# Bias tiles on GpSimd's queue and low-rank weights one head pair earlier, in a two-layer hybrid attention kernel

## The chip, the cores and the metric

The kernel runs on one core of one Trainium2 chip. The metric is device time in microseconds of one execution, as the median of several runs. The engines named below are PE (TensorE, matrix products and transposes), DVE (VectorE), ACT (ScalarE), POOL (GpSimd) and SP (SyncE). SP computes nothing here: it issues transfers, in the order of its instruction stream. POOL both computes and issues transfers.

## The reference

Two layers over 512 latent tokens on a grid 64 wide and 256 context tokens, all of width 1024, in float32. Layer 0 has two groups of eight heads side by side: latent attention with low-rank queries and keys, and two-dimensional neighbourhood attention. Layer 1 has sliding-window attention. Each layer ends in a SwiGLU. The part in which the change lies, cut to what matters:

```
p = modulate(h) @ w_in
# neighbourhood heads: softmax over near latent keys and all context keys
s_lat = q @ k_near * scale + rel_bias[:, row offset, column offset]   # outside the window: -1e30
s_ctx = q @ k_ctx * scale
o_na  = softmax([s_ctx, s_lat]) @ [v_ctx, v_near]
# latent heads
q = rms_norm(p[:, :256], q_norm) @ w_q_up          # 8 heads of 64 + 32 (rotated)
c = rms_norm(p[:, 256:384], kv_norm)
o_mla = softmax((q_nope @ w_uk @ c + q_rope @ k_rope) * scale) @ c @ w_uv
```

## The kernel before

Activations lie with features on partitions and 768 tokens (512 latent, 256 context) along the row. A float32 product is made from three products of high and low parts: `load_w` (L301) fetches a weight into a buffer `wr`, lets ACT write the high part `wh`, and DVE, or POOL where an engine is given, subtract it for the low part `wl`. The transfer is on SP in each case; only the subtraction follows that argument.

After the input projections (`projections`, L1010) the neighbourhood heads run as four pairs p = 0 to 3 (`na_jobs`, L1157). A pair has three jobs: context queries, latent query blocks 0 and 1, blocks 2 and 3. `attend` (L652) runs the front of a job (scores, `take` at L536 with the bias and the row minimum on DVE, `exps` at L532 on ACT) together with the back of the job before it (transposes L482, copies L473 and L474, products with the values L528). Between them it runs steps of the side work: `beside` appends a generator, and `step` (L634) takes the next piece with a lower priority.

For each pair, `nb_tiles` (L944) fetches four bias tiles of 384 KB: for each of the two heads, one with tag `nb` (query blocks 0 and 1; two buffers) and one with tag `b` (blocks 2 and 3; one of 24 buffers that most tiles share). All of them are issued on SP. For pairs 0 and 2 `mix` (L1148) moves parts of the values of two pairs into one tile, with four transfers of 64 KB.

The side work of a pair is set by `ORDER`: "2" and "3" are `split_pair` (L1029), which makes the operands of pairs 2 and 3 with casts, subtractions and moves within the chip; "n" is `latent_norms` (L1072); "m" is `mla_prepare` (L1077), whose first step loads and splits the three low-rank weights `w_ukv` (512 KB), `w_qr` (256 KB) and `w_qn` (512 KB), and whose later steps make the keys, values and queries of the latent heads with them (`pair_ups`, `values`, `up`: the products at L317 to L320 and L738 to L740). `STEPS` allows 2, 3, 4 and 4 steps per job in the four pairs.

The three `wr` buffers serve the scores too: in the neighbourhood heads every fourth tile of exponentials is put into one (`PT`).

The order on each engine isn't that of the program. Every instruction gets a priority in program order, shifted by a number for side work, and a planner, which keeps a timeline of its own, writes each engine's stream (`SCHED`). At run time an engine takes its stream in order and stands where a semaphore isn't there.

Of the kernel before, what the change touches and what calls it, by code (L numbers as in the profile page):

```python
# [51 lines left out]
KEEP = 1  # L52
OUTQ = 1
E1, EF = 1, 1
ORDER = ("2", "n3", "m", "")
AFTER = "012k5r678"
PACE = (3, 3, 3, 3, 5, 5, 5, 6, 5, 5, 3, 2)
KC = (1, 1, 0)
# [40 lines left out]
def hybrid_kernel(ctx: ExitStack, tc, I, out):  # L99
# [6 lines left out]
    def T(tag, shape, dt=F32):  # L106
        count[0] += 1
        if tag not in SIZES:
            return sb.tile(shape, dt, tag=tag, name=f"{tag}_{count[0]}", bufs=BUFS.get(tag, 1))
        n = int(np.prod(shape[1:]))  # L110
        t = sb.tile([P, SIZES[tag] // (2 if dt == mybir.dt.bfloat16 else 4)], dt, tag=tag, name=f"{tag}_{count[0]}",
                    bufs=BUFS[tag])[: shape[0], :n]
        if len(shape) == 3:
            t = t.rearrange("p (a b) -> p a b", a=shape[1])
        return t

    def B(dt=F32, tag="b"):
        return T(tag, [P, NT], dt)
# [12 lines left out]
    V, S, G, PE = nc.vector, nc.scalar, nc.gpsimd, nc.tensor  # L131

    def dma(o, i, eng=None):
        return (eng or nc.sync).dma_start(f(o), f(i))

    def f(ap):
        return ap.bitcast(F32) if ap.dtype == F32R else ap

    silu, marks = [], {}

    def behind(ins, *before):

        for x in before:
            tc.add_manual_dep(ins.ins, x.ins.name, mybir.DependencyInfo(mybir.DependencyClass.NoSync,
                              mybir.DependencyReason.DATA), reason="products in one run")
        return ins
# [154 lines left out]
    def load_w(src, kt, m, eng=None, tag=None, after=()):  # L301

        r = T("wr", [P, kt * m])
        dma(r, src)
        h, lo = (B(F32R, tag)[:, : kt * m] if tag else T(x, [P, kt * m], F32R) for x in ("wh", "wl"))
        behind(S.copy(h, r), *after[:1])  # L306
        behind((G if eng else V).tensor_tensor(lo, r, f(h), op=ALU.subtract), *after[1:])  # L307
        return tuple(x.rearrange("p (k m) -> p k m", k=kt) for x in (h, lo))
# [30 lines left out]
    def split(src, eng=None, dst=None):  # L339

        p, n = src.shape
        h, lo = dst or (B(F32R), B(F32R))
        marks["cast"] = S.copy(h[:p, :n], src)  # L343
        marks["split"] = (eng or V).tensor_tensor(lo[:p, :n], src, f(h[:p, :n]), op=ALU.subtract)
        return h, lo
# [335 lines left out]
    def new_q(tag="st"):  # L681
        return [B(F32R, tag) for _ in range(2)]

    def new_k(tag="st"):
        return [(B(F32R, tag), B(F32R, tag)) for _ in range(2)]
# [184 lines left out]
    for k in range(KT):  # L870
        i = int(k > 5)
# [67 lines left out]
    def beside(gen):  # L939
        side_work.append(gen)  # L940
        return gen


    def nb_tiles(p):  # L944
        ts = {}
        for i in range(2):
            for s in range(2):
                ts[s, i] = B(tag=("nb", "b")[i])
                behind(dma(ts[s, i], I["nb"][2 * p + s, i]), marks["start"])
        cut = (slice(0, 512), slice(256, 768), slice(256, 768), slice(0, 512))  # L950
        return [lambda n, s=s: ts[s, n // 2][:, cut[n]] for s in range(2)]

    def put_rope(t, tabs, swap, rows=P, scale=1.0, tag="b", eng=None):
        def use(src, c):
            if c is LATS:
                rope(t[:rows, c], src, tabs, swap, scale, tag, eng)
            else:
                S.activation(t[:rows, c], src, AF.Copy, scale=scale)

        return use  # L960
# [68 lines left out]
    def split_pair(p):  # L1029

        tag = ("b", "st")[p - 2]
        q, k = raws[2 * p - 4 : 2 * p - 2]
        sets.append((new_q(tag), new_k(tag)))
        up, dn = slice(0, 64), slice(64, 128)
        t0, t1 = sets[p][0]
        S.copy(t0[:, :NT], q)
        lo = q.bitcast(F32R)
        V.tensor_tensor(lo, q, f(t0[:, :NT]), op=ALU.subtract)
        yield
        dma(t1[up, :NT], t0[dn, :NT])  # L1040
        dma(t1[dn, :NT], lo[dn])
        dma(t0[dn, :NT], lo[up])
        (h0, l0), (h1, l1) = sets[p][1]
        S.copy(h0[:, :NT], k)
        V.tensor_tensor(l0[:, :NT], k, f(h0[:, :NT]), op=ALU.subtract)
        yield
        for x, y in ((h0, h1), (l0, l1)):
            dma(y[up, :NT], x[dn, :NT])
            dma(y[dn, :NT], x[dn, :NT])
            dma(x[dn, :NT], x[up, :NT])  # L1050
        yield

    def finish(po, sums, nq):
        finish_pair(po, sums, nq)
        yield

    def cut(w, a, m):
        return w[0][:, :, a : a + m], w[1][:, :, a : a + m]

    def up(w, mov, use):  # L1060
        for c in (LATS, CTXS):
            o = banks([c], PQ)
            mm3(o, w, mov)
            use(*o[0])
            yield

    VM, KR, QR, KA, QA, ready = [], [], [], [], ([], []), []
    kn, qn, wu = [], [], {}
# [3 lines left out]
    def latent_norms():  # L1072
        groups = [(lat_raw[2:], 2), (lat_raw[:2], 0)]
        yield from gained(groups)
        wu["ckv"], wu["cq"] = groups

    def mla_prepare():  # L1077
        wu["kv"] = load_w(I["w_ukv"], 2, 512, G)
        w = load_w(I["w_qr"], 2, 256, G)
        wu["qn"] = load_w(I["w_qn"], 2, 512, G)  # L1080
        KR.extend(split(kr[0][:32, :NT], V))
        yield
        yield from pair_ups(0)
        for i in range(2):
            t = B()
            yield from up(cut(w, i * P, P), wu["cq"], put_rope(t, rope0, SWAP8, scale=MLA_SCALE, eng=V if "r" in EV and i == 0 else None))
            QR.append(split(t, V))
            if i == 0:
                ready.append(latent_operands(0))

    def pair_ups(p):
        kn.append(B())
        qn.append(B())
        wk = wu["kv"]
        yield from up(cut((wk[0][:, 0:1], wk[1][:, 0:1]), p * P, P), wu["ckv"], put(kn[p]))
        yield from up(cut(wu["qn"], p * P, P), wu["cq"], put(qn[p], scale=MLA_SCALE))
        if p % 2 == VP:
            yield from values(p - VP)
# [16 lines left out]
    def latent_operands(h):  # L1115
        p, s = divmod(h, 2)
        r, u = NOPE[s], USED[s]
        rr = slice(32 * (h % 4), 32 * (h % 4) + 32)
        if p < 2:
            if p == 0:  # L1120
                KA.append([T("st", [P, NT], F32R) for _ in range(2)])
            QA[s].append([T("st", [P, NT], F32R) for _ in range(2)])
            for t in [*(KA[s] if p == 0 else ()), *QA[s][p]] if s else ():
                (V if "z" in EV else G).memset(f(t[:32]), 0.0)
            if p == 0:
                for i in range(2):
                    dma(KA[s][i][ROPE[s]], KR[i][:32])
        (ka, kc), (qa, qb) = KA[s], QA[s][p % 2]
        for x, (hi, lo) in ((kn[p], (ka, kc)), (qn[p], (qa, qb))):
            S.copy(hi[r], x[r])  # L1130
            (V if "l" in EV and p < 1 else G).tensor_tensor(lo[r], x[r], f(hi[r]), op=ALU.subtract)
        for t, x in zip((qa, qb), QR[h // 4]):
            if "d" in EV:
                dma(t[ROPE[s]], x[rr])
            else:
                G.dma_start(t[ROPE[s]], x[rr])

        def scores(o, q, keys):
            q = slice(q * P, (q + 1) * P)
            PE.matmul(o, qa[u, q], ka[u, keys], start=True, stop=False)  # L1140
            PE.matmul(o, qb[u, q], ka[u, keys], start=False, stop=False)
            PE.matmul(o, qa[u, q], kc[u, keys], start=False, stop=True)

        return scores
# [12 lines left out]
    def na_jobs():  # L1157
        for p in range(4):
            if p == 3:
                lower[0] = L3  # L1160
            for x in ORDER[p]:
                beside(split_pair(int(x)) if x in "23" else {"n": latent_norms, "m": mla_prepare}[x]())
            rate[0] = STEPS[0][p], BG[p]
            if p % 2 == 0:
                mix()
            po = B()
            sums, mins = T("sm", [P, 6, 2]), T("sm", [P, 6, 2])
            hs, near = [], nb_tiles(p)
            for s in range(2):
                t1, ks = sets[p]  # L1170
                hs.append(Head(s, stacked_scores(t1[s], ks[s]), keys_of(VN[p], s, VX[p]), None, near[s], -LOWEST, sums, mins))
            yield from pair_jobs(hs, po, True, finish(po, sums, 6))
            while len(sets) < min(p + 2, 4):
                step()
            ON.append(po)

    for i, _ in enumerate(projections()):
        n, r = PACE[i // 8], i % 8
# [411 lines left out]
    first_w, kv = soon, soon[:2]  # L1590
# [239 lines left out]
```

## Time and profile before

| | |
|---|---|
| median of 3 runs | 1559.12 us (1555.52 to 1559.58) |
| profiled execution | 1558.19 us |
| its span | 1556.3 us |
| granted TensorE clock, mean | 0.996 |
| moved from and to HBM | 187 MB read, 23 MB written |

The span cut into 40 slices of 38.9 us, each digit the busy share in tenths, the last row the share of the 16 transfer engines:

```profile
DVE  4799867676868687777768676789967779678685
ACT  4532677674555242432424335457856455354453
POOL 0021043110101102012021122470012000000001
...
DMA  9674632013634545537465494110214223323222
```

The neighbourhood pairs run from about 165 to 246 us, which is the fifth to the seventh digit. Transfers go out there from SP's and POOL's queues. A row of the waits reads: who waited, at which line, for whom, total, times, longest.

### The profile page before, as it was taken

To read this page: it belongs to the slowest core of one execution; us is meant where nothing else is said; L and a number is where in the kernel's file an instruction comes from. 1 tells how busy PE (TensorE), PEld (TensorE's weight loads), DVE (VectorE), ACT (ScalarE), POOL (GpSimd) and SP (SyncE) were. 2 spreads that over 40 slices of the span, in tenths; PEclk is the share of its full clock that TensorE was granted. 3 is DMA by queue.
4 is the path that set the end of the run, shared out by engine and by line. 5 is a ranking of instruction groups with operands and counts; after the bars stand their busy time and mean duration, and the time that the engine had idled before them with its cause. 6 is when DMAs were issued, how large, how long until landed. Compare 5 with 4: busy or idle time off the path is not lost.

```text
span 1556.3 us, 26589 instructions
## 1 busy us (share of the span) xinstructions
PE 1529.0 (98%) x10048; PEld 1374.9 (88%) x10048; DVE 1176.5 (76%) x2408; ACT 768.0 (49%) x1531; POOL 217.0 (14%) x269
## 2 busy tenths in 40 slices
PE   9999999999999999999999999999999999999998
PEld 8788877877999898999999988877789899899998
DVE  4799867676868687777768676789967779678685
ACT  4532677674555242432424335457856455354453
POOL 0021043110101102012021122470012000000001
PEclk9999999999999999999999999999999999999999
DMA  9674632013634545537465494110214223323222
GB/s 321 249 226 142 161 125 65 11 63 138 227 128 139 206 134 182 205 118 288 142 249 187 150 358 139 55 41 1 90 57 167 63 91 126 107 84 131 88 94 89
DMA packets 79073, 219.39 MB, mean 141 GB/s; under 512 B 10720, under 2 KB 17888, under 8 KB 78944
## 3 DMA queue, kind: packets, MB, share of 16 engines
q1 hardware_dynamic: 61280, 147.42, 28.6%
q0 software_dynamic: 16512, 68.69, 12.4%
q8 instruction: 79, 1.29, 0.3%
q10 hardware_dynamic: 1152, 1.57, 0.3%
q14 instruction: 50, 0.41, 0.1%
HBM read 186.97 MB, written 23.07 MB: 135 GB/s over the span
## 4 chain that ended last, share of the span: by engine, by line
PE 88%; DVE 7%; ACT 2%; issue 2%; DMA 1%; POOL 0%; DVEq 0%; ACTq 0%; POOLq 0%
PE pss L1401 5%; PE pss L1400 5%; PE pss L1399 5%; PE pso L528 5%; PE pss L320 4%; PE pss L317 4%; PE pss L319 4%; PE psd L317 4%; PE psd L320 4%; PE psd L319 4%; PE pst L317 3%; PE pst L320 3%; PE pst L319 3%; PE pst L1401 3%; PE pst L1399 3%; PE pst L1400 3%
## 5 line engine op out<-in xcount | busy, mean ns | idle before, releaser
L306 ACT CAST wh<-wr 128x1024 fp32r<-128x1024 f32 (+2 forms) x148 | 115.5, 795 | 224.2 <-DMA wr<-in_w_dn_dram 35.0
L307 DVE TENSOR_TENSOR wl<-wr,wh 128x1024 fp32r<-128x1024 f32 (+2 forms) x145 | 130.9, 910 | 80.6 <-ACT wh L306 76.3
L534 ACT ACTIVATE p<-p,sm 128x512 f32<-128x512 f32 (+3 forms) x144 | 105.0, 730 | 25.8 <-DVE sm L538 25.2
L1399 PE MATMUL pss<-b,wh 128*128 128x384 f32 (+1 forms) x346 | 107.7, 312 | 0.5 <-ACT b L343 0.5
L1400 PE MATMUL pss<-b,wh 128*128 128x384 f32 (+1 forms) x346 | 107.8, 312 | 0.0
L1401 PE MATMUL pss<-b,wl 128*128 128x384 f32 (+1 forms) x346 | 107.0, 311 | 0.0
L319 PE MATMUL psd<-b,wh 128*128 128x512 f32 (+2 forms) x254 | 88.6, 349 | 0.0
L273 DVE CUSTOM_DVE_ANT_0 p<-rope,cond 128x1024 bf16<-128x1024 f32 x64 | 76.8, 1219 | 11.4 <-DMA rope<-in_mod_w_dram 11.2
L317 PE MATMUL psd<-b,wh 128*128 128x512 f32 (+2 forms) x214 | 79.1, 370 | 2.8 <-ACT pl L474 2.2
L528 PE MATMUL pso<-ph,b 128*64 128x256 f32 (+1 forms) x384 | 77.9, 362 | 1.0 <-DVE ph L473 0.9
L528 PE MATMUL pso<-pl,b 128*64 128x256 f32 (+1 forms) x384 | 78.4, 363 | 0.0
L320 PE MATMUL psd<-b,wl 128*128 128x512 f32 (+2 forms) x214 | 77.5, 363 | 0.0
L1401 PE MATMUL pst<-b,wl 128*128 128x384 f32 (+1 forms) x226 | 70.6, 313 | 1.5 <-DVE wl L1387 1.5
L1386 ACT CAST wh<-pl 128x512 fp32r<-128x512 f32 x78 | 44.9, 619 | 53.6 <-PE pss L1400 22.7
L1399 PE MATMUL pst<-b,wh 128*128 128x384 f32 (+1 forms) x226 | 70.7, 313 | 0.6 <-ACT p L1449 0.6
L263 POOL DMA_DIRECT2D rope<-in_mod_w_dram x48 | 25.6, 533 | 323.0 <-DVE mod L273 312.1
L1400 PE MATMUL pst<-b,wh 128*128 128x384 f32 (+1 forms) x226 | 70.5, 312 | 0.0
L1386 ACT CAST wh<-wr 128x1024 fp32r<-128x1024 f32 x39 | 41.0, 1051 | 57.7 <-PE pst L1400 14.8
L319 PE MATMUL pss<-b,wh 128*128 128x256 f32 (+3 forms) x216 | 68.4, 316 | 0.0
L317 PE MATMUL pss<-st,wh 128*128 128x512 f32 (+2 forms) x198 | 67.5, 341 | 0.3 <-ACT wh L306 0.3
L320 PE MATMUL pss<-st,wl 128*128 128x512 f32 (+2 forms) x198 | 67.5, 341 | 0.1
L1399 PEld LDWEIGHTS pss<-b,wh 128*128 128x128 f32 x346 | 65.0, 188 | 1.1 <-ACT b L343 0.8
(606 smaller groups left out, 5290.7 us busy)
## 6 DMA issues: line engine op xcount, KB each, us to landing
wr<-in_w_gu_dram SPq DMA_DIRECT2D x88, 512.0 KB, 4.1
rope<-in_mod_w_dram POOLq DMA_DIRECT2D x48, 512.0 KB, 3.9
wr<-in_w_dn_dram SPq DMA_DIRECT2D x73, 256.0 KB, 2.9
wr<-in_w_out_dram SPq DMA_DIRECT2D x32, 512.0 KB, 3.9
p<-home POOLq DMA_DIRECT2D x40, 384.0 KB, 5.6
home<-p POOLq DMA_DIRECT2D x40, 384.0 KB, 5.9
wr<-in_w_in_dram SPq DMA_DIRECT2D x21, 512.0 KB, 3.9
ph<-in_mod_w_dram SPq DMA_DIRECT2D x24, 256.0 KB, 2.8
```

Source lines behind the costliest of these rows:

```text
L273: behind(V.tensor_tensor_reduce(out=T("p", [P, D], mybir.dt.bfloat16), in0=w, in1=cond[:, v, :], op0=ALU.mult, op1=ALU.add, scale=1.0, sca ...
L306: behind(S.copy(h, r), *after[:1])
L307: behind((G if eng else V).tensor_tensor(lo, r, f(h), op=ALU.subtract), *after[1:])
L317: ins = PE.matmul(o, wh[:, k], mh[:, c], start=first and k == 0, stop=False)
L319: PE.matmul(o, wh[:, k], ml[:, c], start=False, stop=False)
L320: PE.matmul(o, wl[:, k], mh[:, c], start=False, stop=last and k == n - 1)
L528: ins = PE.matmul(o[64 * i : 64 * i + 64, c], v(kt), t, start=n == 0, stop=n == len(moving[i]) - 1)
L534: S.activation(p[:, c], p[:, c], AF.Exp, bias=nm, scale=-1.0, accum_out=dn)
L1386: S.copy(h, t)
L1399: PE.matmul(o, wh, xh, start=first and k == 0, stop=False, skip_group_check=not first)
L1400: PE.matmul(o, wh, xl, start=False, stop=False, skip_group_check=not first)
L1401: PE.matmul(o, wl, xh, start=False, stop=k == 3, skip_group_check=not first)
```

## The change

Three things. The bias tiles of pairs 1 and 2, and the `nb` tiles of pair 3, are issued by POOL; those of pair 0 and the `b` tiles of pair 3 stay on SP. `nb_tiles` is called ahead of `mix`, so that the bias tiles come first in program order where both are called, and the `b` tiles take their buffers ahead of the tile of `mix` and of the output tile `po`. The three low-rank weights are loaded, cast and split in the first three side steps of pair 1, one each, instead of together in the first step of pair 2.

```diff
-ORDER = ("2", "n3", "m", "")
+ORDER = ("2", "wn3", "m", "")
...
-                behind(dma(ts[s, i], I["nb"][2 * p + s, i]), marks["start"])
+                behind(dma(ts[s, i], I["nb"][2 * p + s, i], G if 0 < p < 4 - i else None), marks["start"])
...
+    def mla_weights():
+        for x, name, m in (("kv", "w_ukv", 512), ("qr", "w_qr", 256), ("qn", "w_qn", 512)):
+            wu[x] = load_w(I[name], 2, m, G)
+            yield
+
     def mla_prepare():
-        wu["kv"] = load_w(I["w_ukv"], 2, 512, G)
-        w = load_w(I["w_qr"], 2, 256, G)
-        wu["qn"] = load_w(I["w_qn"], 2, 512, G)
+        w = wu["qr"]
         KR.extend(split(kr[0][:32, :NT], V))
...
             for x in ORDER[p]:
-                beside(split_pair(int(x)) if x in "23" else {"n": latent_norms, "m": mla_prepare}[x]())
+                beside(split_pair(int(x)) if x in "23" else {"n": latent_norms, "w": mla_weights, "m": mla_prepare}[x]())
             rate[0] = STEPS[0][p], BG[p]
+            near = nb_tiles(p)
             if p % 2 == 0:
                 mix()
             po = B()
             sums, mins = T("sm", [P, 6, 2]), T("sm", [P, 6, 2])
-            hs, near = [], nb_tiles(p)
+            hs = []
```

## The prediction

> **What bounds the kernel now.** First the page: busy times, then the chain that ended last.
>
> ```profile
> span 1556.3 us, 26589 instructions
> ...
> PE 1529.0 (98%) x10048; PEld 1374.9 (88%) x10048; DVE 1176.5 (76%) x2408; ACT 768.0 (49%) x1531; POOL 217.0 (14%) x269
> ...
> PE 88%; DVE 7%; ACT 2%; issue 2%; DMA 1%; POOL 0%; DVEq 0%; ACTq 0%; POOLq 0%
> ```
>
> PE is the bound and the change takes no matmul away. It can win holes in PE's row, 1556.3 - 1529.0 = 27.3 us in the whole program, and the slow clock behind them. Next, PE's waits over the whole program, longest first:
>
> ```profile
> PE psd L317 <- ACT pl L474: 2.2, 1, 2.2
> PE pst L1401 <- DVE wl L1387: 1.5, 1, 1.5
> ```
>
> The longest one lies in the neighbourhood attention, where the changed lines run. Busy time there in steps of 2 us (PE, PEld, DVE, ACT, POOL, clock, DMA share, GB/s), and from the chain the same work at slow and at full clock:
>
> ```profile
> 202.00:204.00 2.00, 0.45 (x4) 0.24 (x3) 0.88 (x1) 2.00 (x8) 2.00 (x1) 1.00 1.00 360
> 204.00:206.00 2.00, 1.11 (x5) 0.66 (x7) 2.00 (x3) 2.00 (x8) 0.30 (x1) 1.00 0.78 303
> 206.00:208.00 2.00, 2.00 (x18) 1.67 (x18) 2.00 (x6) 2.00 (x6) 0.00 (x0) 0.61 0.02 9
> 208.00:210.00 2.00, 2.00 (x12) 1.24 (x9) 1.01 (x3) 2.00 (x6) 0.00 (x0) 0.54 0.66 241
> ```
> ```profile
> 205.86 3.17 PE pso L528 x20
> 209.03 1.44 PE pst L482 x8
> ...
> 212.43 1.88 PE pso L528 x20
> ...
> 216.99 0.87 PE pst L482 x8
> ```
>
> PE is dry for 1.55 + 0.89 = 2.44 us, and then the granted clock falls to 0.61 and 0.54: the twenty products take 3.17 instead of 1.88 us, the eight transposes 1.44 instead of 0.87, together 1.86 us. **The hole costs 2.44 + 1.86 = 4.30 us.** Why it opens, on ACT, DVE and POOL:
>
> ```profile
> 196.57 0.19 ACT L534 ACTIVATION_READ_ACCUMULATOR p<-p,sm 128x1 f32 x1
> 200.82 1.05 ACT L306 CAST wh<-wr 128x1024 fp32r<-128x1024 f32 x1 [4.05 <-DMA wr<-in_w_ukv_dram]
> ```
> ```profile
> 190.70 0.95 DVE L344 TENSOR_TENSOR b<-b,b 128x768 fp32r<-128x768 f32 x1
> ...
> 203.12 1.99 DVE L344 TENSOR_TENSOR b<-b,b 128x768 fp32r<-128x768 f32 x1 [1.81 <-ACT b L343]
> ...
> 206.24 0.67 DVE L538 CUSTOM_DVE_ANT_0 p<-pss,nb 128x512 f32<-128x512 f32 x1
> ```
> ```profile
> 201.94 2.35 POOL L307 TENSOR_TENSOR wl<-wr,wh 128x1024 fp32r<-128x1024 f32 x1 [55.62 <-ACT wh L306]
> 212.54 1.28 POOL L307 TENSOR_TENSOR wl<-wr,wh 128x512 fp32r<-128x512 f32 x1 [8.24 <-ACT wh L306]
> ...
> 215.56 2.38 POOL L307 TENSOR_TENSOR wl<-wr,wh 128x1024 fp32r<-128x1024 f32 x1
> ```
>
> ACT stands 4.05 us in front of the cast of the first low-rank weight, which has not landed. The exponentials and copies queued behind it are late; DVE then waits 1.81 us for ACT, and its subtraction takes 1.99 instead of 0.95 us because POOL's split runs until 204.29. The next score that DVE takes starts at 206.24, 4.93 us after it stopped. Why the weight is late, from SP's queue, its landing time, and SP's own waits (184 to 191, then 201 to 208 us):
>
> ```profile
> 194.39 1.01 SPq L134 DMA_DIRECT2D nb<-in_nb_dram  x1
> 195.45 0.44 SPq L134 DMA_DIRECT2D wr<-in_w_ukv_dram  x1
> ```
> ```profile
> wr<-in_w_ukv_dram SPq DMA_DIRECT2D x1, 512.0 KB, 5.3
> ```
> ```profile
> SPq L134 <- DMA st<-st: 4.3, 1, 4.3
> ...
> SPq L134 <- DVE sm L538: 5.6, 1, 5.6
> ```
>
> The load is issued at 195.45, behind a bias tile and behind the moves of the fourth pair's operands, for which SP stood 4.3 us, and lands 5.3 us later, as ACT's wait ends. A bias tile of the last pair holds the same queue 5.6 us.
>
> **The change part by part.** *Weights.* Three loads, three casts and three splits move from the third pair's first step to the second pair's first three steps.
>
> ```profile
> L306 ACT CAST wh<-wr 128x1024 fp32r<-128x1024 f32 (+1 forms) x3 | 2.7, 905 | 4.1 <-DMA wr<-in_w_ukv_dram 4.1
> ```
> ```profile
> 179.00:194.00 15.00, 14.98 (x126) 11.96 (x126) 14.96 (x40) 12.47 (x36) 0.00 (x0) 1.00 0.88 234
> 194.00:246.00 52.00, 47.92 (x359) 38.78 (x356) 35.49 (x84) 36.32 (x87) 21.36 (x17) 0.97 0.41 131
> 180.00:186.00 6.00, 6.00 (x57) 5.09 (x57) 5.96 (x18) 5.16 (x17) 0.00 (x0) 1.00 1.02 292
> ```
>
> If they come in time, the hole of 4.30 us goes: the products, scores and transposes that wait there have their data. What they meet instead is the second pair, about 179 to 194 us, with DVE full (14.96 of 15) and ACT 2.53 us free. The casts are 2.7 us: between nothing and 2.7 us of delay, and 0.3 taken, since nearly all fits. The splits are 2.35 + 1.28 + 2.38 = 6.01 us of POOL, empty there; one that meets a subtraction of DVE costs up to 2.4 us. In the trace one met, at 1.99 - 0.95 = 1.04 us; I take one again, now where DVE has no slack, and half of it reaches PE: 0.5. What is late next: nothing long; PE is dry for 52 - 47.92 = 4.08 us from 194 to 246, of which 1.64 lie outside the hole.
>
> *Bias of the second to fourth pair.* Ten transfers, 4 + 4 + 2, leave SP for POOL.
>
> ```profile
> 174.72 0.68 DVE L538 CUSTOM_DVE_ANT_0 p<-pss,nb 128x512 f32<-128x512 f32 x1
> ...
> 181.25 0.69 DVE L538 CUSTOM_DVE_ANT_0 p<-pss,nb 128x512 f32<-128x512 f32 x1
> ```
> ```profile
> 177.68 1.07 SPq L134 DMA_DIRECT2D nb<-in_nb_dram  x2
> ```
> ```profile
> p<-home POOLq DMA_DIRECT2D x40, 384.0 KB, 5.6
> ...
> nb<-in_nb_dram SPq DMA_DIRECT2D x8, 384.0 KB, 4.8
> ```
> ```profile
> 241.72 0.57 POOL L263 DMA_DIRECT2D rope<-in_mod_w_dram  x1
> ```
>
> On POOL an issue takes 0.57 us, so 5.7 us in all beside 21.36 us of work; SP is rid of ten issues of about 0.5 us. The same 384 KB lands in 5.6 us from POOL's queue, 4.8 from SP's: 0.8 us later. Against that, the second pair's tiles are free at 175.40, when the last take of the first pair has read them, and SP issued them at 177.68: POOL can be 2.3 us earlier, so the first take at 181.25 isn't delayed. A bias tile that must wait for its buffer now holds POOL: behind it stand the weight splits and, in the last two pairs, the subtractions for the latent heads. What hides this is POOL's empty time, 30.6 of 52 us from 194 to 246; where a split is wanted at once, the cover is gone and a wait like the 5.6 us above falls on whoever needs it. Value: 0, bounds -1 (SP's share of the lateness) to +2. [...]
>
> *First pair's bias ahead of the value moves.*
>
> ```profile
> 165.46 2.46 SPq L134 DMA_DIRECT2D b<-b  x4
> 168.04 1.00 SPq L134 DMA_DIRECT2D b<-in_nb_dram  x2
> ```
> ```profile
> 175.33 0.69 DVE L538 CUSTOM_DVE_ANT_0 p<-pss,b 128x512 f32<-128x512 f32 x1
> ```
>
> The two tiles go out some 2.5 us sooner, but are first read at 175.33, 7.3 us after their issue, by a DVE that was busy just before: worth 0. The moves go 1.0 us later; bounds 0 to +1.
>
> **Sum.** -4.30 + 0.3 + 0.5 = -3.5 us. The profiled execution took 1558.19 us (span 1556.3, the rest around it), so 1554.7. It lies 0.93 us below the median of the three runs, 1559.12, from which the same step gives 1555.6. I forecast 1555.0, between them. About 0.3%, 4.7 us, is what a measurement of this kernel can tell from no change; the hole is just below that.
>
> **The rivals.** *1. The wait moves along.* The planner places casts by when it thinks data lands, and from 180 to 186 us the transfer engines are full. Then ACT stands in the second pair as it stood in the third, for about the same 4.05 us, at the same price: 0, so 1558 to 1559. For it: the DMA share, and that by the code the second and third load reuse buffers which the first pair's scores hold until they are transposed. Against it: the new steps come ahead of the fourth pair's moves, and the queue is shorter by the bias. It is also the case in which the loads are placed late and the change doesn't do what it says.
>
> *2. Slower: the weight buffer as a trap.* The scores share the three weight buffers.
>
> ```profile
> 185.96 0.68 DVE L538 CUSTOM_DVE_ANT_0 wr<-pss,nb 128x512 f32<-128x512 f32 x1
> ```
>
> With the weights loaded in the second pair, its take at 185.96 writes the buffer that the first weight passes through. Landing 5.3, cast 1.05 and split 2.35 make 8.7 us, so the load must go out by 177.3. Each us after that holds DVE, with all its takes behind. The hold of 4.93 us cost 2.44 of PE: PE lives 2.5 us on what it has. A load at 182.2 thus costs the 4.30 that the change removes; later ones make it slower. Behind the 4.3 us wait of the moves, at 182.2 + 4.3 = 186.5 by estimate, the hold is 9.2 us: 9.2 - 2.5 + 1.86 - 4.30 = +4.3, 1562.5 to 1563.4; the end of this case is some 3 us more. For it: SP skips nothing that waits. Against it: by the code that buffer was last used by the projections and is free long before.
>
> *3. More is won.* Low-rank products that are ready earlier fill the other 1.64 us of holes: 1558.19 - 4.30 - 1.64 = 1552.3; for it that PE takes any product that is ready, against it that those holes are chains of DVE and ACT.
>
> **How the numbers follow.** Forecast (1553 to 1557) 0.40, the wait moved along 0.24, slower 0.14, more won 0.22. Faster by over 0.3% is below 1554.4: rival 3 and a third of the forecast, 0.35. Slower is above 1563.8: half of rival 2 and a little for orders further on that the planner changes, 0.10. Within: 0.55. The range goes from 1549.0 (rival 3, less most of the 3.6 us by which the fastest run, 1555.52, lies under the median) to 1564.0, within rival 2.
>
> **What would show it.** Right: no wait of ACT for a low-rank weight, no wait of PE at L317 for L474, clock 1.00 all through the pairs, more PE busy time between 194 and 246, and bias tiles issued from POOL as soon as the takes free them. Wrong: an ACT wait for a weight in the second pair (rival 1), a DVE take into a weight buffer waiting for POOL's split (rival 2), or POOL's subtractions late behind a bias tile. A changed order after the attention, with holes of its own, would make the size wrong with the mechanism right.

## The result and the profile after

The changed kernel takes 1566.53 us (median of 6 runs, 1562.20 to 1567.87), the kernel before 1558.89 us in the same series (1555.52 to 1561.25). The ratio is 1.0041 with a 95% interval of [1.0028, 1.0054]: slower by 0.41%, some 6.4 us (the two medians lie 7.6 us apart). The forecast was 1555.0 with a range up to 1564.

The page of the changed kernel, three rows that answer to those of before:

```profile
span 1563.9 us, 26587 instructions
...
PE 1531.1 (98%) x10048; PEld 1377.8 (88%) x10048; DVE 1177.1 (75%) x2408; ACT 768.4 (49%) x1531; POOL 222.5 (14%) x279
...
PE 85%; DVE 7%; ACT 3%; DMA 2%; issue 2%; POOL 0%; SPq 0%; DVEq 0%; ACTq 0%; POOLq 0%
```

The span grew by 7.6 us and PE's busy time by 2.1, so PE idles 5.5 us more and runs longer on the same matmuls. In the chain PE went from 88% to 85%, and ACT and DMA have a point more each. Where it happens is told by windows: from, to, length, then the busy time of PE, PEld, DVE, ACT and POOL with the count of instructions, PE's granted clock, the share of the transfer engines, GB/s. First the kernel before, over the four pairs' first part, the end of the low-rank attention and what follows it:

```profile
160.00:210.00 50.00, 47.00 (x348) 38.90 (x347) 39.77 (x105) 35.84 (x92) 2.35 (x1) 0.97 0.71 205
320.00:350.00 30.00, 28.86 (x216) 22.93 (x215) 25.39 (x76) 23.64 (x59) 3.62 (x2) 1.00 0.22 78
350.00:400.00 50.00, 47.99 (x299) 41.05 (x298) 36.42 (x66) 22.48 (x40) 1.62 (x3) 1.00 0.46 164
```

Then the changed kernel, in the same windows:

```profile
160.00:210.00 50.00, 42.19 (x303) 34.82 (x301) 33.23 (x86) 30.96 (x75) 10.33 (x11) 0.90 0.73 185
320.00:350.00 30.00, 27.42 (x195) 21.74 (x194) 26.56 (x69) 22.72 (x52) 7.62 (x4) 0.94 0.00 1
350.00:400.00 50.00, 47.99 (x313) 39.28 (x312) 33.38 (x69) 25.32 (x50) 0.57 (x1) 1.00 0.50 173
```

From here on **lost time** of PE is its idle time in a window plus its busy time times (1 - granted clock), summed over windows of 10 us, whose clocks are less rounded than these. Between 160 and 210 us it went from 4.3 us (3.0 idle, 1.3 by the clock) to 11.6 us (7.8 and 3.8); between 320 and 350 us from 1.1 to 4.1 us; from 400 to 600 us both lose 0.5. From 600 to 1550 us the changed kernel's trace loses less, 10.7 us instead of 13.2; the change touches nothing there, and why is open. So there are two places where it loses more.

**The first is the second pair.** The old hole at 202 us is gone, and a larger one stands at 185 us:

```profile
180.00:185.00 5.00, 5.00 (x49) 4.19 (x47) 4.47 (x14) 1.45 (x5) 0.00 (x0) 1.00 1.01 287
185.00:190.00 5.00, 0.32 (x3) 0.12 (x1) 1.06 (x3) 0.55 (x1) 0.00 (x0) 0.79 1.05 220
190.00:195.00 5.00, 2.96 (x13) 2.67 (x14) 0.97 (x3) 5.00 (x14) 3.24 (x2) 0.50 0.91 201
195.00:200.00 5.00, 5.00 (x35) 3.74 (x34) 2.26 (x5) 2.25 (x7) 1.43 (x3) 0.69 0.95 268
```

PE does 0.32 us of work in the five us from 185, and the clock is at half speed behind it, while the transfer engines are full (1.05). The waits of 160 to 255 us (who, at which line, for whom: total, times, longest) name three engines that stand together:

```profile
ACT wh L306 <- DMA wr<-in_w_ukv_dram: 8.0, 1, 8.0
...
DVE wr L538 <- POOL wl L307: 6.9, 1, 6.9
PE pst L482 <- ACT p L534: 6.5, 2, 5.7
```

ACT stands at the cast of the first low-rank weight, which hasn't landed. DVE stands at a take that writes scores into the very buffer which this weight passes, until POOL has split it. PE's dry time is put down to ACT. ACT stops at 181.45, and PE has work until 185.32. Both of PE's waits up to 195 us, 5.73 and 0.99 us, end with an exponential that stands behind the cast:

```profile
191.05 0.47 PE L482 MATMUL pst<-ident_r,p 128*128 128x128 f32 x1 [5.73 <-ACT p L534]
```

DVE's hold ends none of PE's waits from 180 to 200 us. The timeline of SP's queue shows when the load went out, and that of POOL's instructions when the bias did (start, duration, what, count; in brackets the idle time before it and its releaser):

```profile
172.79 6.68 SPq L134 DMA_DIRECT2D b<-b  x4
179.51 0.58 SPq L134 DMA_DIRECT2D wr<-in_w_ukv_dram  x1
```

```profile
172.50 0.59 POOL L134 DMA_DIRECT2D nb<-in_nb_dram  x1 [26.11 <-DVE sm L538]
174.60 0.54 POOL L134 DMA_DIRECT2D nb<-in_nb_dram  x1 [1.50 <-DVE sm L538]
175.13 1.06 POOL L134 DMA_DIRECT2D b<-in_nb_dram  x2
```

POOL sent the second pair's four bias tiles at 172.5 to 176.2, where SP had sent the `nb` pair at 177.68 and the `b` pair at 179.41 before: some 4 to 5 us earlier, right among the moves of 192 KB within the chip. The list of transfers from 160 to 215 us (KB each, median us from issue to landing), first of the kernel before, then of the changed one:

```profile
b<-b SPq DMA_DIRECT2D x7, 192.0 KB, 3.2
```

```profile
b<-b SPq DMA_DIRECT2D x7, 192.0 KB, 6.7
...
wr<-in_w_ukv_dram SPq DMA_DIRECT2D x1, 512.0 KB, 9.9
```

The moves land twice as late, SP stands 4.2 us for one of them, the load goes out behind them, and it needs 9.9 us instead of the 5.3 of the third pair.

A slow landing isn't the whole of it. Two runs told below have the weights in the same place and the second pair's bias on SP. Their load goes out 1.3 and 1.9 us later and lands at 188.72 and 189.37, against 189.45 in the changed kernel, so at most 0.7 us earlier by the clock. Yet ACT stands at the cast for 3.7 and 4.5 us in them, not for 8.0, because it comes there later: three exponentials and two copies stand ahead of the cast in its stream which stand behind it in the changed kernel. First the run with the second pair's bias back on SP, from the first of the two copies to the cast; then the changed kernel, from the cast to that copy:

```profile
182.49 0.57 ACT L474 COPY ph<-psd 128x512 f32<-128x512 f32 x1
...
184.65 0.36 ACT L612 COPY b<-pso 128x256 f32<-128x256 f32 x1
188.72 1.04 ACT L306 CAST wh<-wr 128x1024 fp32r<-128x1024 f32 x1 [3.71 <-DMA wr<-in_w_ukv_dram]
```

```profile
189.45 1.04 ACT L306 CAST wh<-wr 128x1024 fp32r<-128x1024 f32 x1 [8.00 <-DMA wr<-in_w_ukv_dram]
...
192.36 0.57 ACT L474 COPY ph<-psd 128x512 f32<-128x512 f32 x1
```

These five take 2.5 us (182.49 to 185.01). In DVE's stream, too, the take into the weight's buffer comes sooner: DVE reaches it at 186.06 in the changed kernel, at 189.44 and 189.26 in the two others. So the planner's order has its part in the long stand. The landing has the rest: the first of the two traces runs some 1.1 us behind the changed kernel's by 165 us, so by the work done its load lands 1.9 us earlier.

**The second is the end of the low-rank attention**, 150 us after anything that the change touches. In ACT's stream four casts of operands (L1133, L1193, L1194) stand ahead of the exponential of one score tile that stood before them in the kernel before (at 327.71 us there):

```profile
335.90 0.93 ACT L534 ACTIVATE wr<-wr,sm 128x768 f32<-128x768 f32 x1
```

```profile
336.00:338.00 2.00, 0.54 (x4) 0.30 (x3) 2.00 (x5) 2.00 (x5) 0.43 (x1) 1.00 0.00 0
338.00:340.00 2.00, 2.00 (x9) 1.67 (x8) 2.00 (x6) 1.81 (x7) 0.00 (x0) 0.51 0.00 0
340.00:342.00 2.00, 2.00 (x9) 1.44 (x9) 2.00 (x9) 0.00 (x0) 0.00 (x0) 0.64 0.04 8
```

1.46 us dry, then 2 x 0.49 + 2 x 0.36 = 1.7 us by the clock. The planner wrote another order here, presumably since its own timeline came out otherwise.

### The profile page after: what moved, and what is told of

Read it like the earlier page. It is cut to its first block, busy times and chain, and to the rows that moved or that the text cites. A ratio compares the mean times of both kernels' runs of the same rounds, so it can differ in the third digit from the quotient of the medians.

```text
span 1563.9 us, 26587 instructions
## 1 busy us (share of the span) xinstructions
PE 1531.1 (98%) x10048; PEld 1377.8 (88%) x10048; DVE 1177.1 (75%) x2408; ACT 768.4 (49%) x1531; POOL 222.5 (14%) x279
## 4 chain that ended last, share of the span: by engine, by line
PE 85%; DVE 7%; ACT 3%; DMA 2%; issue 2%; POOL 0%; SPq 0%; DVEq 0%; ACTq 0%; POOLq 0%
PE pss L1405 5%; PE pss L1404 5%; PE pss L1403 5%; PE pso L528 5%; PE psd L317 4%; PE psd L320 4%; PE pss L317 4%; PE psd L319 4%; PE pss L320 4%; PE pss L319 4%; PE pst L317 3%; PE pst L320 3%; PE pst L319 3%; PE pst L1405 3%; PE pst L1403 3%; PE pst L1404 3%
## 5 line engine op out<-in xcount | busy, mean ns | idle before, releaser
L482 PE MATMUL pst<-ident_r,p 128*128 128x128 f32 x346 | 61.4, 280 | 8.6 <-ACT p L534 7.1
```

## The experiments

Twelve kernels were run, each timed beside the kernel before (ratios are to it, with 95% intervals). Theories by letter: W, the weights' new place makes the loss; Q, the bias on GpSimd's queue does; P, the order that the planner writes does; M, the second hole costs what it shows; others are told with their run. All edits are to the changed kernel, unless said. The numbers are gathered in a table at the end.

**Weights only** (bias on SP, where before had it):

```diff
-                behind(dma(..., G if 0 < p < 4 - i else None), marks["start"])
+                behind(dma(..., None), marks["start"])
...
-            near = nb_tiles(p)
...
-            hs = []
+            hs, near = [], nb_tiles(p)
```

> The change's weights alone: loaded, cast and split in the first three steps of the second pair; all bias tiles on SP and fetched where the kernel before fetches them. Theory W (the loss is the weights': ACT stands at a cast whose load hasn't landed): ACT waits 4 us or more for the first weight inside the second pair, PE is dry there for 4 us or more, time 1563 to 1568 us. Theory Q (the loss is the queue's: bias tiles sent sooner from POOL fill the transfer engines, and so the weight is late): without them the weight lands in some 5 us, the hole of before is gone and no new one opens, 1554 to 1557 us.

Measured: 1.0038 [1.0024, 1.0052]. Its waits from 160 to 255 us:

```profile
ACT wh L306 <- DMA wr<-in_w_ukv_dram: 4.5, 1, 4.5
DVE wr L538 <- POOL wl L307: 3.6, 1, 3.6
```

The weights alone make the kernel slower, as W said: the load lands in 8.0 us in the second pair even with the bias on SP, where Q expected 5. The hole is half as long as in the changed kernel, though (lost time 6.5 instead of 11.6). But the profiled execution took 1561.84 us, 2.8 less than the median of 1564.60, so the trace shows less than the usual run loses.

**Bias only** (weights back in the third pair):

```diff
-ORDER = ("2", "wn3", "m", "")
+ORDER = ("2", "n3", "m", "")
...
     def mla_prepare():
+        for _ in mla_weights():
+            pass
         w = wu["qr"]
```

> The change without its weights: ten bias tiles on POOL's queue, the first pair's ahead of the value moves, the three weights in the first step of the third pair as before. Theory W: the hole of before at 202 us stays or shrinks a little, since a bias tile no longer stands ahead of the load, 1555 to 1560 us. Theory Q: the moves land late and hold SP, 1563 us or more.

Measured: 1.0024 [1.0011, 1.0038]. Its transfers and its wait in the old place:

```profile
wr<-in_w_ukv_dram SPq DMA_DIRECT2D x1, 512.0 KB, 9.0
```

```profile
PE psd L317 <- ACT pl L474: 3.8, 1, 3.8
```

The bias on POOL costs something alone too, less than Q expected. In this trace it is again by way of the weight: in the third pair it now lands in 9.0 us instead of 5.3, and PE's old wait of 2.2 us became 3.8. The trace is of the slowest of twelve executions, 1566.28 us against a median of 1561.86, so these are large values.

**Order only** (as bias only, and all bias on SP; what is left is `nb_tiles` ahead of `mix`):

```diff
-                behind(dma(..., G if 0 < p < 4 - i else None), marks["start"])
+                behind(dma(..., None), marks["start"])
```

> Only the call of the bias tiles ahead of the value moves, everything on SP and the weights as before. Theories W and Q: no difference, 1557 to 1561 us. Rival P (any edit makes the planner write other streams further on, and that moves the time by several us): more than 2.5 us off either way.

Measured: 0.9991 [0.9977, 1.0004]. The first pair's bias ahead of the moves costs nothing.

**Weights ahead of all pairs** (weights only, with the three loads made before the first pair begins):

```diff
-ORDER = ("2", "wn3", "m", "")
+ORDER = ("2", "n3", "m", "")
...
     dense[0] = False
+    for _ in mla_weights():
+        pass
     attend(na_jobs())
```

> Bias tiles as in the kernel before; the three weights are loaded, cast and split ahead of all pairs, while the last projections run and the transfer engines are idle (DMA share 0.00 to 0.01 from 155 to 165 us). Theory W: no wait of ACT for a low-rank weight, the hole of before is gone and none takes its place, 1553 to 1556 us. Rival C (the work itself costs, casts on ACT, splits on POOL against DVE, products that come sooner): no gain, 1558 us or more.

Measured: 1.0000 [0.9986, 1.0013]. The first load goes out at 128.11 us, among the projections, and lands in 3.2 us. No engine stands for a weight, and the lost time of 160 to 210 us falls to 1.0 us, so the prediction's hole is gone as it was meant to go. The 3.3 us by which this is below before's 4.3 didn't reach the time: the profiled execution lost more in other places (1.7 us by the clock from 120 to 160, 1.0 more before 120, and 1.5 more in the second hole), only the last of which belongs to its order. The time is near rival C's (1558 or more), not within W's (1553 to 1556). By the interval, taking the hole away is worth at most 2.2 us, and not the 4.30 that its dry time and its slow clock show.

**Weights ahead, bias on POOL** (as the last, with the bias as in the changed kernel):

> Weights loaded and split ahead of all pairs, bias tiles of the second to fourth pair on GpSimd's queue and the first pair's ahead of the value moves; the low-rank attention keeps the order of the kernel before. Theory W (the weights' place makes the loss, the queue of the bias costs nothing by itself): no wait of ScalarE for a weight, 1553.5 to 1556. Theory Q (bias tiles on GpSimd's queue go out together with the moves and delay what lands, with whatever weights): moves of 192 KB land after more than 6 us in the second pair, and 1558 or more.

Measured: 1555.57 us, 0.9984 [0.9973, 0.9995]. This is the one version that beats both kernels, by little. Its list of transfers:

```profile
b<-b SPq DMA_DIRECT2D x7, 192.0 KB, 6.3
```

Q was right that the moves land late with the bias on POOL (6.3 us), and wrong that this costs by itself: with no weight behind them, PE waits for none of them from 165 to 215 us (its longest wait there, 1.6 us, ends with an exponential). Its lost time, 10.7 us up to 600 us, is that of before (10.9); where its gain of some 2 us lies isn't shown by that sum.

**Second pair's bias back on SP** (the rest as in the changed kernel, with its order at the end):

```diff
-                behind(dma(..., G if 0 < p < 4 - i else None), marks["start"])
+                behind(dma(..., G if 1 < p < 4 - i else None), marks["start"])
```

> The changed kernel with the second pair's bias tiles back on SyncE; those of the third and fourth pair stay on GpSimd's queue, and the order of ScalarE in the low-rank attention is that of the changed kernel. Theory Q (the second pair's bias tiles, pulled 5 us earlier by GpSimd's queue, share the DMA engines with the moves and the first weight and make them late): moves of 192 KB land in about 3.5 us again, the first weight in 8 us or less, ScalarE stands 4 to 5 us for it instead of 8, TensorE loses 6 to 7 us of work at 160 to 210 us instead of 11.6, and 1562 to 1564.5. Rival P (the weight lies behind the moves whatever the bias does): landing near 9.9 us, 11 us lost, 1566.

Measured: 1561.32 us, 1.0013 [1.0002, 1.0025], against 1.0041 [1.0028, 1.0054] of the changed kernel: 0.28% or 4.4 us for four bias tiles. Transfers and waits:

```profile
b<-b SPq DMA_DIRECT2D x7, 192.0 KB, 3.4
```

```profile
ACT wh L306 <- DMA wr<-in_w_ukv_dram: 3.7, 1, 3.7
...
DVE wr L538 <- POOL wl L307: 2.8, 1, 2.8
```

The signs that Q named came: the moves land in 3.4 us again, the load in 7.9, ACT stands 3.7 us instead of 8.0, DVE 2.8 instead of 6.9, and PE loses 5.0 us from 160 to 210 instead of 11.6. But Q's way is not the only one in the trace. Of the 4.3 us that ACT stands less, some 2.5 are the five instructions that the planner put ahead of the cast here, as shown above, and the rest is the landing. So the 4.4 us are the price of the four issues on POOL together with the order that came with them, and no run prices the two apart. Nor is it the price of these tiles wherever they are: weights only has them on SP as well and is at 1.0038.

**Cast on POOL** (ACT no longer touches a low-rank weight):

```diff
-        behind(S.copy(h, r), *after[:1])
+        behind((G.tensor_copy if eng is G else S.copy)(h, r), *after[:1])
```

> The changed kernel with the cast of each low-rank weight's high half on GpSimd, in front of its subtraction there, and no longer on ScalarE; the low-rank attention keeps the order of the kernel before, which by theory M is worth 3 us by itself. Theory A (ScalarE standing at the cast makes the hole in the second pair): no dry time over 1 us at 185 to 200 us, 1555 to 1558. Theory R (the buffer is the trap: a take of VectorE for scores into the weight's buffer waits for GpSimd's split): VectorE waits 7 us or more for the split, TensorE dry by 4 us or more, and 1562 to 1566.

Measured: 1556.38 us, 0.9989 [0.9978, 1.0000], the time that theory A named. The load lands in 8.6 us, at 187.8, which is 1.6 us earlier than in the changed kernel, and DVE still stands at the take; the waits and windows:

```profile
ACT wr L534 <- DVE sm L538: 5.7, 2, 4.5
DVE wr L538 <- POOL wl L307: 4.7, 1, 4.7
```

```profile
185.00:190.00 5.00, 5.00 (x49) 4.16 (x48) 1.30 (x3) 1.75 (x5) 2.04 (x2) 1.00 1.04 230
190.00:195.00 5.00, 3.49 (x25) 2.52 (x25) 3.62 (x10) 2.40 (x6) 4.29 (x5) 1.00 1.00 230
195.00:200.00 5.00, 4.21 (x31) 2.98 (x28) 5.00 (x10) 3.66 (x10) 3.08 (x2) 1.00 0.92 264
```

With the cast off ACT, ACT works until 187.6 and then stands 4.5 us for DVE's take. PE works all through 185 to 190, the clock stays at 1.00, and the lost time is 3.2 us. A's sign itself was missed, since PE is dry for 1.5 us from 190 to 195. Nor is the gain A's alone: DVE's hold is also 2.2 us shorter than in the changed kernel, and the end has the order without the second hole. What the trap costs by itself can be read here: for a hold of 4.7 us on DVE, PE is dry for 2.3 us from 185 to 200.

**Exponentials ahead of the casts** at the end of the low-rank attention, in the changed kernel, and with the weights ahead of all pairs. Both have this edit, in which `ran` collects the exponentials and `hold` is, from the sixth head on, one of the last of them:

```diff
-            S.copy(hi[r], x[r])
+            behind(S.copy(hi[r], x[r]), *hold)
...
-        S.copy(rows(h), half_blocks(src))
-        S.copy(h[:, CTXS], src[:, CTXS])
+        behind(S.copy(rows(h), half_blocks(src)), *hold)
+        behind(S.copy(h[:, CTXS], src[:, CTXS]), *hold)
...
+            hold[:] = [ran[-2]] if h >= 5 else []
...
```

> The changed kernel with one order put back: in the low-rank attention the casts of the next head's operands stand behind the exponentials of the last scores on ScalarE, as in the kernel before; the pairs are as in the changed kernel. Theory M (a second hole, at 336 to 342 us of the changed kernel, made by that order: TensorE dry 1.46 us and a clock of 0.51 and 0.64 behind it, about 3.2 us): 3 us less than the changed kernel, 1562.5 to 1564, and the hole of the second pair (ScalarE standing 8 us for the first weight) as it is. Theory P (the hole in the pairs alone makes the loss): 1566, as the changed kernel.

> Weights loaded and split ahead of all pairs, bias tiles on SyncE as before, and the exponentials of the last scores ahead of the casts in the low-rank attention. Theory M with H (each hole is worth what its dry time and slow clock show: 4.3 us for that of the kernel before in its third pair): both holes are gone, 1553.5 to 1556, so 3 us less than the run with the weights ahead alone (1557.8). Rival C (the time of a hole is filled by work that is late later, so none of it comes back): 1557.5 to 1559.

Measured: 1.0039 [1.0021, 1.0057] and 0.9995 [0.9984, 1.0006], so no change from their bases (1.0041 and 1.0000): the times that P and C named, not M's. The hole itself went (lost time of 320 to 350 us from 4.1 to 0.3, and from 2.6 to 0.8), but the casts that were held back are then late: from 350 to 400 us the two lose 6.0 and 3.9 us instead of 2.0. PE waits there, in the waits of 320 to 400 us of the first:

```profile
PE pss L317 <- ACT st L1195: 1.8, 1, 1.8
```

**Casts ahead of the exponential, in the kernel before**: the order of the second hole alone, by one dependence.

```diff
-        S.activation(p[:, c], p[:, c], AF.Exp, bias=nm, scale=-1.0, accum_out=dn)
+        ran.append(S.activation(p[:, c], p[:, c], AF.Exp, bias=nm, scale=-1.0, accum_out=dn))
...
-        S.copy(rows(h), half_blocks(src))
+        casts.append(S.copy(rows(h), half_blocks(src)))
         S.copy(h[:, CTXS], src[:, CTXS])
+        if len(casts) == 3:
+            behind(ran[82], casts[-1])
```

> The kernel before with a single order added: in the low-rank attention one exponential of ScalarE (the fifth-buffer scores of 128x768 at 327.71 us) stands behind the cast of the third head pair's rows, so that four casts stand ahead of it as in the changed kernel; the pairs, the weights and the bias are the kernel before's. Theory M (that order makes the hole at 336 to 342 us of the changed kernel and costs what it shows): TensorE loses 2.6 us or more in 320 to 350 us instead of 1.1, and the time is 1.5 to 3.5 us above the kernel before's, 1560.5 to 1562.5. Rival N (the order alone costs nothing: the hole is made by what the late pairs leave): 1558.5 to 1559.7.

Measured: 0.9999 [0.9988, 1.0009]. That is rival N's time, not M's. The order does make a hole here, but a small one: 2.1 us lost from 320 to 350 instead of 1.1, with no slow clock, where the changed kernel loses 4.1. By the interval it costs at most 1.4 us. What the larger hole costs is not measured by this.

**Scores of the neighbourhood pairs never in a weight buffer**:

```diff
-PT = (("p", "p", "p", "wr"), ...
+PT = (("p", "p", "p", "p"), ...
```

> The changed kernel with one name changed in the table of the score buffers: a score of the first four pairs never takes a weight's buffer. The order in which the program is laid out then has the three weights go out among the projections, before the first pair. Theory W (the late place of the weights makes the hole in the second pair, not the bias on GpSimd's queue): ScalarE stands for no weight, VectorE waits for no split, 2 us or less lost at 180 to 210 us, 1554 to 1557. Rival B (the scores need the fifth buffer: with one fewer, VectorE's takes wait for transposes in each pair): over 1560 with no wait for a weight.

Measured: 1561.83 us, 1.0017 [1.0007, 1.0027]: over 1560 with no wait for a weight, as rival B said, and not W's time. The loads went out at 126.49 us and landed in 3.3, and nobody stands for a weight or a split; the 1.9 us lost from 180 to 210 are within what W allowed. But in the waits of 160 to 255 us ACT now stands for DVE's takes:

```profile
ACT p L534 <- DVE sm L538: 13.1, 10, 4.4
```

With weights ahead and bias on POOL that is 3.8 us in 6 waits. So B has its part, the scores having fewer buffers. But the end has yet another order, with 6.4 us lost from 320 to 400. The two aren't told apart.

**Weights from the first pair on**:

```diff
-ORDER = ("2", "wn3", "m", "")
+ORDER = ("w2", "n3", "m", "")
```

> The changed kernel with the weights fetched and split from the first pair on, one pair earlier still; their loads go out among the projections. The low-rank attention keeps the order of the changed kernel, with five casts ahead of an exponential at 336 us. Both theories: no hole at 185 to 200 us. Theory M (the order of those casts costs what the hole at 336 to 342 us shows): 3 us more than the run with weights ahead and the bias on GpSimd's queue (1555.6), so 1558 to 1559.5. Rival N (that hole is paid for later in any order, as the two runs with the exponentials moved ahead suggest): 1555 to 1557.

Measured: 1570.59 us, 1.0071 [1.0057, 1.0085], the slowest of all, and neither theory was tested by it. The loads did go out at 126.61 us. But the moves for a later pair came out of the side work late: on SP's queue the last of the second group were issued at 199.62, and PE stood for one:

```profile
206.08 0.58 PE L729 MATMUL pss<-b,b 128*128 128x256 f32 x1 [3.89 <-DMA b<-b]
```

A step put in front of a pair's side work delays the rest of that work.

All runs together. "Load" is when the first low-rank weight was issued and how long it took to land; "ACT" and "DVE" how long each stood for it or for its split; then PE's lost time in three ranges. All but the times and ratios are of one profiled execution each, in us.

| kernel | time | ratio, interval | load | ACT | DVE | 160–210 | 320–400 | 0–600 |
|---|---|---|---|---|---|---|---|---|
| before | 1558.89 | 1 | 195.45, 5.3 | 4.1 | 0 | 4.3 | 3.1 | 10.9 |
| changed | 1566.53 | 1.0041 [1.0028, 1.0054] | 179.51, 9.9 | 8.0 | 6.9 | 11.6 | 6.2 | 20.1 |
| weights only | 1564.60 | 1.0038 [1.0024, 1.0052] | 181.39, 8.0 | 4.5 | 3.6 | 6.5 | 6.1 | 15.7 |
| bias only | 1561.86 | 1.0024 [1.0011, 1.0038] | 197.20, 9.0 | 4.7 | 0 | 6.6 | 4.6 | 17.3 |
| order only | 1557.11 | 0.9991 [0.9977, 1.0004] | 195.62, 6.6 | 4.3 | 0 | 5.0 | 3.2 | 10.7 |
| weights ahead | 1557.80 | 1.0000 [0.9986, 1.0013] | 128.11, 3.2 | 0 | 0 | 1.0 | 4.6 | 10.9 |
| weights ahead, bias on POOL | 1555.57 | 0.9984 [0.9973, 0.9995] | 126.48, 3.3 | 0 | 0 | 3.4 | 2.6 | 10.7 |
| second pair's bias on SP | 1561.32 | 1.0013 [1.0002, 1.0025] | 180.81, 7.9 | 3.7 | 2.8 | 5.0 | 4.6 | 12.3 |
| cast on POOL | 1556.38 | 0.9989 [0.9978, 1.0000] | 179.20, 8.6 | 0 | 4.7 | 3.2 | 2.0 | 9.5 |
| exponentials first | 1565.60 | 1.0039 [1.0021, 1.0057] | 178.97, 9.2 | 7.0 | 5.9 | 9.7 | 6.3 | 18.5 |
| weights ahead, exponentials first | 1558.21 | 0.9995 [0.9984, 1.0006] | 126.16, 3.3 | 0 | 0 | 1.7 | 4.7 | 8.9 |
| casts first, in before | 1558.83 | 0.9999 [0.9988, 1.0009] | 195.78, 6.3 | 3.5 | 0 | 2.5 | 4.0 | 11.6 |
| scores not in `wr` | 1561.83 | 1.0017 [1.0007, 1.0027] | 126.49, 3.3 | 0 | 0 | 4.9 | 6.4 | 14.9 |
| weights from the first pair | 1570.59 | 1.0071 [1.0057, 1.0085] | 126.61, 3.6 | 0 | 0 | 11.2 | 4.6 | 19.3 |

The last column goes with the time: the kernels that lose up to 11.6 us lie within 0.16% of before, the one with 12.3 is 0.13% slower, and the six with 14.9 or more are slower by 0.17% to 0.71%. It isn't exact, since it is one execution against a median.

## Why the prediction was wrong

**What held.** PE was the bound and the old hole came from ACT's cast waiting for the weight: loaded ahead of all pairs, the hole is gone (lost time from 4.3 to 1.0 us). The first pair's bias ahead of the moves is worth 0, as forecast (0.9991, and the interval takes in 1). The rule for the trap in rival 2 held to 0.1 us once the landing is put right: 9.9 + 1.05 + 2.35 = 13.3 us ahead of the take at 185.96 is 172.7; the load went out at 179.51, 6.8 us late, and DVE stood 6.9. The agreement owes something to luck, since DVE came to that take at the old time: with the second pair's bias on SP it came 3.4 us later.

**The step that failed** is the sum's -4.30, "If they come in time, the hole of 4.30 us goes", with the landing of 5.3 us behind it. That landing was a row of the third pair, used for a load in the second, where the prediction's own row had the transfer engines at 1.02. There it lands in 8.0 us with all bias on SP, ACT stands 4.5 us for it, and this alone turns the change into 1.0038. The size of the term failed as well. With the weights ahead of all pairs the hole does go, and the gain is at most 2.2 us by the interval (1.0000), or some 2.5 us with the bias on POOL (0.9984). So 4.30 us in PE's row were not 4.30 us of time; where the rest goes is open.

**The term that was mis-sized** is the bias, "Value: 0, bounds -1 ... to +2". By the two ratios, putting the second pair's four tiles back on SP saves 4.4 us in the changed kernel, over twice the upper bound. The 2.3 us by which POOL could be earlier was counted as a small gain; it was 4 to 5 us. It put 1.5 MB among the moves and the weight, and with it came an order in which ACT meets the cast five instructions sooner; which of the two cost more isn't shown. With no weight behind them the same tiles cost nothing (0.9984). The parts don't add up: 0.38% for the weights alone, 0.24% for the bias and the order of its calls, 0.41% for all. The prediction priced them one by one, and what they do to each other was not in the sum.

**Rivals as alternatives.** Rival 1 (ACT stands in the second pair) and rival 2 (the weight buffer as a trap) were given 0.24 and 0.14 as if one excluded the other. They came together. Rival 1's price, 0 for a stand of some 4.05 us, was too low: in weights only ACT stands 4.5 us, and the kernel is 0.38% slower. Rival 2's allowance, "PE lives 2.5 us on what it has", fits the run with the cast on POOL, where a hold of 4.7 us left PE dry for 2.3. In the changed kernel the dry time is ACT's: PE lived 3.9 us after ACT had stopped, then was dry for 4.68 + 2.04 = 6.7 us from 185 to 195, and the clock behind cost 2.96 x 0.50 + 5.00 x 0.31 = 3.0 more. Rival 1's 0 for the sum came nearer than the forecast all the same, but it leaves out that POOL sends the second pair's tiles 4 to 5 us earlier (172.5 to 176.2 us, where SP had sent them from 177.68 on).

**Splits and casts** (+0.3 and +0.5) can't be told from the rest. Rival 3 (1552.3) was reached by no version. That "PE takes any product that is ready" was the author's estimate of the planner's order; at run time PE stood 5.73 us in front of one transpose at 185 us in the changed kernel.

**The second hole.** A changed order after the attention was named as something that could make the size wrong. It is there in the trace, with 3.0 us more lost than before from 320 to 350 us. But this order in the kernel before, where it makes a smaller hole, costs no time that can be measured, and moving the exponentials ahead only moved the lost time behind it. What it costs in the changed kernel, with the clock at 0.51 and 0.64 behind it, stays open.

Open too: why weights only (1.0038) is 0.25% slower than the run with the second pair's bias on SP (1.0013), though ACT stands at the weight about as long in both (4.5 and 3.7 us); why the planner put the first load behind the moves in the second pair, though its buffer was free (with the scores kept out of `wr` it placed it among the projections by itself), and why the versions that load there, with no wait for a weight in any, still reach from 0.9984 to 1.0017 without the one whose moves are late.

## What to carry to other kernels

Price a transfer that is moved by how transfers land where it goes, with what the same change puts beside it there, not by the row of the place that it leaves (8.0 us here, where that row said 5.3). Before a load goes earlier, look which buffer it passes and who writes that buffer next: a late load holds that engine too (here DVE, for 6.9 us). Compare where the waiting instruction stands in its engine's stream, not only when the data lands: here the load landed at nearly the same time in three kernels, and the stand in front of it went from 3.7 to 8.0 us. Parts of a change need not add up, so time each alone and all together. And closing a hole in the busiest engine's row may win less than the hole shows: with the load in the stage before, where it landed in 3.2 us, the hole was gone and the time was that of before.

## What the hardware showed that was not expected

**The same 512 KB landed in 3.2 us and in 9.9.** Sent by SP each time, it took 3.2 to 3.6 us among the projections; in the third pair 5.3 to 6.6 with the bias on SP and 9.0 with it on POOL; in the second 7.9 to 8.0 with that pair's bias on SP and 8.6 to 9.9 with it on POOL. In the changed kernel a move of 192 KB went from 3.2 to 6.7 us. The transfer engines were busy to 0.92 while the load was in flight in the kernel before (5.3 us) and to 1.03 in the changed one (9.9 us). So tiles that POOL sent went with a later landing of what SP sent; by what means, no run here shows.

**The same dry time has two prices.** In the changed kernel 1.46 us dry at 336 us was followed by clocks of 0.51 and 0.64. With the second pair's bias on SP the same order makes the same 1.46 us dry, some 5 us earlier, and the clock stays:

```profile
330.00:332.00 2.00, 0.90 (x8) 0.66 (x7) 2.00 (x3) 2.00 (x6) 1.08 (x1) 1.00 0.00 0
332.00:334.00 2.00, 1.64 (x12) 1.46 (x12) 2.00 (x7) 1.98 (x6) 0.00 (x0) 1.00 0.00 0
334.00:336.00 2.00, 2.00 (x17) 1.23 (x17) 2.00 (x7) 0.49 (x2) 0.00 (x0) 1.00 0.03 8
```

Why the clock fell after the one gap and not after its twin, no run here shows. In the run with weights ahead and bias on POOL the clock was 0.83 in a stretch in which PE was never dry:

```profile
150.00:160.00 10.00, 10.00 (x67) 9.64 (x67) 9.61 (x24) 3.38 (x6) 2.34 (x1) 0.83 0.23 75
```

In the kernel before, the clock was 1.00 there. So some 1.7 us of lost time is in one trace and not in another, which is why a hole's worth is better read from timed runs than from one trace's clock.
